# Hybrid encoder block: PSUM banks divided four and four, merge products in both sets by turns, early feature blocks two by two

## The chip, the cores and the metric

The kernel runs on one core of a Trainium2 chip. The metric is the device time of one execution in microseconds (us). Five engines work side by side: TensorE (PE, matrix products and transpositions), VectorE (DVE), ScalarE (ACT), GpSimd (POOL) and SyncE (SP), which here issues the DMAs. Each takes its instructions in the order of its own queue and waits on semaphores for the others. PE accumulates into banks of PSUM; this kernel uses eight tiles of 128 x 512 float32 there.

## The reference

The reference is an encoder block of 1024 tokens and model width 1024: a projection, two attention branches, a gated merge, an output projection, and a SwiGLU feed-forward of width D_FF = 2816. The part that the change touches begins behind the attention branches:

```python
    merged = jax.nn.sigmoid(ga) * (y_a @ w_ba) + jax.nn.sigmoid(gb) * (y_b @ w_bb)
    return merged @ w_o

def swiglu(h, w_gate, w_up, w_down):
    return (jax.nn.silu(h @ w_gate) * (h @ w_up)) @ w_down
```

Around the feed-forward stand a residual sum, an RMS norm ahead of it and one at the end.

## The kernel before

Each float32 operand is split into a high and a low part, and a product of two operand tiles is three matmuls (high by high, high by low, low by high).

**Merge** (`gated`, tile names ppa). There are 32 products: 8 output blocks `o` by 2 token halves, first for branch b (i = 0), then for branch a (i = 1). Each loads its gate from memory into one of four gate tiles (gt), ACT applies the sigmoid, PE makes 12 matmuls into a bank, DVE multiplies gate and bank (L896), and for branch a POOL adds that to the sum (L897), which also frees the gate tile. Branch a runs half 0 mostly first: the last six of its sixteen products are blocks 2 to 7 of half 1. Sums and differences of merged blocks (L905, L912, L913, L1159) and of weights (L1107, L1161, L1163) for the next stage stand on DVE between these.

**Output projection** (po) is done by a Strassen-Winograd scheme of seven block products. Products 1 and 2 accumulate into four banks each (set1, set2), later ones follow in the same sets; products 5 and 3 take a third set of four. `out_add` (L934) adds a finished bank to the residual h. When a row block of h is complete, `norm_f` makes its norm xn_f (L1062, L1064) and stores h.

**Turns** (`turn_f`, tile names ptn_f) transpose xn_f on PE: eight transpositions of a row block into two banks, from which ACT and DVE make the operands b11, b21, b22 and, for row blocks 4 to 7, the sums t (L1082 to L1097). Turns 5, 6 and 7 stand between the first feed-forward products: ahead of products number 0, 2 and 4.

**Feed-forward gate and up** (`product_f`, tile names pg) goes over 11 blocks of 256 features (fp), again with seven block products p in the order 1, 2, 6, 5, 7, 3, 4, each for gate (i = 0) and up (i = 1). One product is 12 matmuls. The result of p = 1 is needed twice: as the first part of p = 2's bank and of p = 6's bank. ACT therefore copies it (L1239) into a second bank. The first four blocks do their p = 1 and p = 2 ahead of the rest, since the operands of the other products are not ready. Of these four, the first N_KEPT keep the p = 1 bank until p = 6; the others ("late") copy p = 1 to a tile in SBUF, let p = 2 accumulate on the same bank, and copy the tile back to a new bank when p = 6 comes. A finished gate block goes through Silu on ACT (L1227); the up block is multiplied in by DVE (L1232). Weights come through raw tiles (five, shared with xn_f), are split by ACT and by DVE or POOL (L112, L113), and wait in eight operand tiles (wop).

**Down projection** (pd, `product_d`) is one more Winograd scheme with sets of four banks.

PSUM for all of this is one pool with two tags: `ps_bank`, six tiles, and `ps_bank_t`, two tiles. The transpositions use ps_bank_t, the feed-forward's products ps_bank except p = 5. A tile is given to a new user when its last user is done.

PE's order is the order in which the program is written. The order on the other engines from the merge to the end of the feed-forward's gate and up part is set by the framework's scheduler, from its own model; from the down projection on it is the written order again.

Of the kernel before, what the change touches and what calls it, by code (L numbers as in the profile page):

```python
# [70 lines left out]
def encoder_block(ctx: ExitStack, tc: tile.TileContext, x, meta, norm_mix, w_in, lq1, lk1, lq2, lk2,  # L71
# [10 lines left out]
    def pool(name, side="left", space=None, bufs=1):  # L82
        kw = {} if space is None else {"space": space}
        if space is not DRAM:
            kw["reuse_waits"] = "tile"
        cm = tc.tile_pool(name=name, bufs=bufs, side=side, **kw)
        p = cm.__enter__()
        return p, lambda: cm.__exit__(None, None, None)
# [5 lines left out]
    def bank(p, tag, name, bufs):  # L94
        return p.tile([P, 512], F32, tag=tag, name=name, bufs=bufs)
# [452 lines left out]
    def branch_mm(ps, w, src, tk):  # L548
        for j in range(4):
            for n, (a, b) in enumerate(((0, 0), (0, 1), (1, 0))):  # L550
                nc.tensor.matmul(ps, w[:, a, j, :], src(j, b, tk),
                                 start=(j == 0 and n == 0), stop=(j == 3 and n == 2))
# [208 lines left out]
    psum3, close_psum3 = pool("psum3", space=PSUM)  # L761
# [1 line left out]


    def ps_bank(name):
        return bank(psum3, "bank", name, 6)

    def ps_bank_t(name):
        return bank(psum3, "bank_t", name, 2)

    pad, close_pad = pool("pad", "right")
    pad.tile([P, PAD // 4], F32, name="pad")
# [83 lines left out]
    def gated(i, o, half, w, src):  # L856
        tk = slice(half * 512, half * 512 + 512)
        gt = ypool.tile([P, 512], F32, tag="gt", name=f"gt_{i}_{o}_{half}", bufs=GT_BUFS)
        nc.sync.dma_start(gt, g_d[8 * i + o][:, tk])
        nc.scalar.activation(gt, gt, AF.Sigmoid)  # L860
        ps = (ps_bank_t if half else ps_bank)(f"ppa_{o}_{half}_{i}")
        branch_mm(ps, w, src, tk)
        return gt, ps, tk

# [2 lines left out]
    for o in range(DC):  # L867
        w = first_w[o] if o < 2 else branch_w(ypool, o, w_bb, "b")
        for half in range(2):
            gt, ps, tk = gated(0, o, half, w, yb)  # L870
            nc.vector.tensor_tensor(merged(o, half), gt, ps, ALU.mult)
        if o in (1, 5):
            load_ya(o // 4)
        if 3 <= o < 6:
            load_wo(*((w11, 0, 0), (w12, 0, 1), (w21, 1, 0))[o - 3])
        if o >= 4:
            right_o(1, o - 4)
            tt_v(w11[:, o - 4], w12[:, o - 4], w11[:, o - 4], ALU.subtract)
        if o == 6:
            ws_a = {0: branch_w(ypool, 0, w_ba, "a", None, nc.vector)}  # L880
        if 2 <= o < 6:
            split_ya(0, o - 2)
# [9 lines left out]
    for n, (o, half) in enumerate(order_a):  # L892
        if o not in ws_a:
            ws_a[o] = branch_w(ypool, o, w_ba, "a", None, nc.vector)
        gt, ps, tk = gated(1, o, half, ws_a[o], ya)
        nc.vector.tensor_tensor(gt, gt, ps, ALU.mult)  # L896
        nc.gpsimd.tensor_tensor(merged(o, half), gt, merged(o, half), ALU.add)  # L897
        if 4 <= n < 8:
            right_o(2, n - 4)
            left_o(1, n - 4)  # L900
        elif 10 <= n < 14:
            left_o(2, n - 10)
        if n in (6, 8, 10, 11):

            tt_v(a21[:, o], a11[:, o], a21[:, o], ALU.subtract)  # L905
        if n == 10:
            w22 = obpools["w22"] = block_pair(2, "m2", F32)[:, 0]
            load_wo(w22, 1, 1)
        if n >= 12:

            j = n - 12
            tt_v(asum[:, j], a22[:, j], a21[:, j], ALU.subtract)  # L912
            tt_v(a11[:, j], asum[:, j], a11[:, j], ALU.add)  # L913
# [18 lines left out]
    def out_add(t, q, ps):  # L932
        cols = slice(q * 512, q * 512 + 512)
        nc.vector.tensor_tensor(h2[t][:, cols], h2[t][:, cols], ps, ALU.add)  # L934

    first, rest, order_pm = (1, 2), (6, 5, 7, 3, 4), (1, 2, 6, 5, 7, 3, 4)
    N_EARLY, N_KEPT = 4, 2
    order_f = [(0, p, i) for p in first for i in range(2)]
    order_f += [(fp, p, i) for fp in range(1, N_EARLY) for i in range(2) for p in first]
    order_f += [(fp, p, i) for fp in range(N_EARLY) for p in rest for i in range(2)]  # L940
    order_f += [(fp, p, i) for fp in range(N_EARLY, NJ) for p in first + rest for i in range(2)]
    nf = len(order_f)
# [116 lines left out]
    def norm_f(t):  # L1059
        xn = raw_tile(f"xn_f{t}")  # L1060
        ss = small.tile([P, 1], F32, tag="ss", name=f"ss_f{t}")
        nc.scalar.activation(xn, h2[t], AF.Square, accum_out=ss)  # L1062
        r = rstd_of(ss, D, P, f"rstd_f{t}")
        nc.vector.scalar_tensor_tensor(xn, h2[t], r, gffn, ALU.mult, ALU.mult)  # L1064
        nc.sync.dma_start(h2_d[t], h2[t])
        xns[t] = xn

    def turn_f(t):
# [5 lines left out]
        for b in range(2):  # L1074
            pt = four(ps_bank_t(f"ptn_f{t}_{b}"))
            for c in range(4):
                k = 4 * b + c
                nc.tensor.transpose(pt[:, c, :], xn[:, k * P:(k + 1) * P], ident)
            pts.append(pt)
            if b or not half:  # L1080
                op = b22 if half else (b11, b21)[b]
                nc.scalar.activation(op[:, 0, :, cols], pt, AF.Copy)  # L1082
                nc.vector.tensor_tensor(op[:, 1, :, cols], pt, f32(op[:, 0, :, cols]), ALU.subtract)
            if not half:
                nc.scalar.copy(four(kept[:, b * 512:b * 512 + 512]), pt)
# [23 lines left out]
    order_t = ((7, 0), (7, 1), (7, 2), (4, 0), (7, 3), (4, 1), (4, 2), (4, 3))  # L1109
    steps_o = [(p, j) for p in (1, 2, 6, 5, 3) for j in range(4)]  # L1110
    set1 = [ps_bank(f"po_1_{u}") for u in range(4)]
    set2 = [(ps_bank, ps_bank_t)[u // 2](f"po_2_{u}") for u in range(4)]
    sets_o = {1: set1, 2: set2, 6: set1}

    def product_o(p, j, u):
        oa, ob = lefts[p, j], rights[p, j]
        for k, (a, b) in enumerate(((0, 0), (0, 1), (1, 0))):
            nc.tensor.matmul(sets_o[p][u], oa[:, a, u * P:(u + 1) * P], ob[:, b, :],  # L1118
                             start=(p in (1, 5) and j == 0 and k == 0),
                             stop=(p in (2, 3) and j == 3 and k == 2), skip_group_check=True)  # L1120
# [8 lines left out]
    def ahead(n):  # L1129

        if n + 8 < 20:
            p, j = steps_o[n + 8]
            right_o(p, j)
            left_o(p, j)
        else:
            right_o((7, 4)[n // 4 - 3], n % 4)
            left_t(*order_t[n - 12])

    for n, (p, j) in enumerate(steps_o):
        if (p, j) == (5, 0):  # L1140
            sets_o[5] = sets_o[3] = [(ps_bank, ps_bank_t)[u // 2](f"po_5_{u}") for u in range(4)]
        last = p in (5, 3) and j == 3
        if p in (5, 3) and j == 2:
            continue
        for u in range(4):
            for k in (2, 3) if last else (j,):
                product_o(p, k, u)
            if (p, j) == (1, 3):

                nc.scalar.copy(set2[u], set1[u])  # L1150
            elif j == 3:

                out_add(u + 4 * (p == 5), int(p > 2), sets_o[p][u])
                if p == 3:
                    norm_f(u)
        for k in (n - 1, n) if last else (n,):
            ahead(k)
            if 4 <= k < 8:
                tt_v(a12[:, k - 4], a12[:, k - 4], asum[:, k - 4], ALU.subtract)  # L1159
            elif 8 <= k < 12:  # L1160
                tt_v(w12[:, k - 8], w22[:, k - 8], w12[:, k - 8], ALU.subtract)  # L1161
            elif 12 <= k < 16:
                tt_v(w21[:, k - 12], w21[:, k - 12], t2[(k - 12) // 2][:, k % 2 * 512:k % 2 * 512 + 512], ALU.subtract)  # L1163
# [134 lines left out]
    sums, sets = {}, {}  # L1298
    BANKS = {1: 1, 6: 1, 7: 1, 4: 1, 2: 2, 5: 5, 3: 5}
# [4 lines left out]
    def product_d(p, j, us_):  # L1304
        oa, ob = ops["d", (p, j)]
        if BANKS[p] not in sets:
            sets[BANKS[p]] = [(ps_bank_t if BANKS[p] > 1 and u > 1 else ps_bank)(f"pd_{p}_{u}") for u in range(4)]
        ps = sets[BANKS[p]]
        for u in us_:
            for k, (a, b) in enumerate(((0, 0), (0, 1), (1, 0))):  # L1310
                nc.tensor.matmul(ps[u], oa[:, a, u * P:(u + 1) * P], ob[:, b, :],  # L1311
                                 start=(p in (1, 2, 5) and j == 0 and k == 0),
                                 stop=(p in (2, 3, 4) and j == NJ - 1 and k == 2), skip_group_check=True)
# [53 lines left out]
    for n in range(nf, len(steps)):  # L1367
        p, j = steps[n][1]
# [3 lines left out]
        if p in LOADS:  # L1372
            at, half, col = LOADS[p]
# [62 lines left out]
```

## Time and profile before

| What | Value |
|---|---|
| Three timed runs | 1477.86, 1481.01, 1481.19 us (median 1481.01) |
| Profiled execution | 1472.57 us, span 1470.8 us |
| Granted TensorE clock, mean of the span | 0.991 |
| Busy: PE, DVE, ACT, POOL | 1439.6, 895.4, 676.0, 474.1 us |
| The output projection begins | 730.36 us |
| The feed-forward's first product begins | 814.46 us |
| Its block products from p = 6 on begin | 876.98 us |
| The down projection begins | 1252.34 us |

The span runs from the first to the last instruction of the profiled execution. A row of a timeline gives start, length, engine, line, operation, output and inputs, form and count, and in brackets the time that the engine stood idle before it and what ended the idling. A row of the waits names engine, tile and line, what it waited for, then the sum, the number and the longest. Tile names in the profile leave the numbers out: pg is any product bank of the feed-forward, wop any weight operand, p the SBUF tile of p = 1.

### The profile page before, as it was taken

What the parts mean: (1) busy time and instruction counts of PE and PEld (TensorE: products, weight loads), DVE (VectorE), ACT (ScalarE), POOL (GpSimd) and SP (SyncE); (2) the same over time, 40 slices, a digit from 0 to 9 for tenths busy, and PEclk for the clock granted to TensorE, in tenths of its full rate; (3) what the DMA queues carried; (4) which work ended last, traced back from release to release, by engine and by line L of the source; (5) the groups of instructions that cost most, each with busy time, mean ns of one, the idle gap of its engine ahead of it and who ended that gap; (6) DMA issues with size and microseconds to landing.
All of it is one profiled execution on the core that took longest, in us unless ns stands there. A gap on an engine that the chain in (4) does not pass through costs nothing.

```text
span 1470.8 us, 20980 instructions
## 1 busy us (share of the span) xinstructions
PE 1439.6 (98%) x7327; PEld 1232.8 (84%) x7327; DVE 895.4 (61%) x1750; ACT 676.0 (46%) x1273; POOL 474.1 (32%) x460
## 2 busy tenths in 40 slices
PE   8999999999999999999899799999999999999997
PEld 7999989988898989888688578888888888888886
DVE  6456326628686878346777835564444443787667
ACT  6356336526455545356246634333333333444454
POOL 4143223313322322222403024555455442000444
PEclk9999999999999999999999899999999999999999
DMA  7333452372524151195232524333333323954343
GB/s 234 90 98 113 118 130 85 77 228 77 145 73 152 66 152 66 43 343 172 95 143 86 165 79 129 123 123 107 108 101 100 102 94 106 347 197 141 125 128 137
DMA packets 158617, 191.01 MB, mean 130 GB/s; under 512 B 16096, under 2 KB 103584, under 8 KB 158512
## 3 DMA queue, kind: packets, MB, share of 16 engines
q1 hardware_dynamic: 158512, 189.68, 40.8%
q8 instruction: 58, 0.95, 0.3%
q14 instruction: 47, 0.39, 0.1%
HBM read 129.14 MB, written 53.94 MB: 124 GB/s over the span
## 4 chain that ended last, share of the span: by engine, by line
PE 82%; DMA 4%; issue 4%; POOL 3%; DVE 3%; ACT 2%; SPq 0%; POOLq 0%; ACTq 0%; DVEq 0%
PE pg L1215 28%; PE pp_g L200 11%; PE pd L1311 8%; PE aps L607 4%; PE po L1118 3%; PE apy L649 3%; PE pp_qb L200 3%; PE pp_va L200 3%; PE pp_ka L200 3%; PE pp_qa L200 3%; POOL oa L113 3%; PE apt L636 2%; PE bpt L338 2%; PE bpy L344 2%; PE bps L313 1%
## 5 line engine op out<-in xcount | busy, mean ns | idle before, releaser
L1215 PE MATMUL pg<-t,wop 128*128 128x512 f32 x1056 | 242.4, 389 | 0.0
L1215 PEld LDWEIGHTS pg<-t,wop 128*128 128x128 f32 x1056 | 198.2, 188 | 41.2
L1311 PE MATMUL pd<-ob,oa 128*128 128x512 f32 x924 | 210.2, 389 | 0.9 <-DVE ob L113 0.5
L113 POOL TENSOR_TENSOR wop<-wf,wop 128x512 fp32r<-128x512 f32 x114 | 153.3, 1345 | 165.5 <-ACT wop L112 153.7
L1311 PEld LDWEIGHTS pd<-ob,oa 128*128 128x128 f32 x924 | 173.3, 188 | 37.6 <-DVE ob L113 0.9
L1215 PE MATMUL pg<-b,wop 128*128 128x512 f32 x792 | 187.9, 395 | 4.0 <-ACT p L1239 2.7
L1215 PEld LDWEIGHTS pg<-b,wop 128*128 128x128 f32 x792 | 150.2, 191 | 37.8 <-ACT p L1239 4.4
L113 POOL TENSOR_TENSOR wl_c<-w_c,wh_c 128x1024 fp32r<-128x1024 f32 x32 | 77.7, 2428 | 162.0 <-ACT wh_c L112 151.8
L112 ACT ACTIVATE wop<-wf 128x512 fp32r<-128x512 f32 x128 | 80.6, 632 | 79.5 <-PE pg L1215 46.8
L618 ACT ACTIVATE as<-as,amn 128x1040 f32<-128x1040 f32 x64 | 74.6, 1165 | 72.6 <-DVE amn L613 72.4
L200 PE MATMUL pp_g<-hT_hi,wh_c 128*128 128x512 f32 x256 | 101.3, 396 | 0.0
L200 PE MATMUL pp_g<-hT_lo,wh_c 128*128 128x512 f32 x256 | 100.9, 394 | 0.0
L200 PE MATMUL pp_g<-hT_hi,wl_c 128*128 128x512 f32 x256 | 100.9, 394 | 0.0
L113 POOL TENSOR_TENSOR oa<-ra,oa 128x512 fp32r<-128x512 f32 x33 | 44.1, 1337 | 170.8 <-ACT oa L112 169.3
L112 ACT ACTIVATE oa<-ra 128x512 fp32r<-128x512 f32 x77 | 48.7, 632 | 106.7 <-PE pd L1311 51.4
L607 PE MATMUL aps<-ak,aq 128*128 128x352 f32 (+1 forms) x384 | 92.6, 326 | 0.0
L987 DVE TENSOR_TENSOR s<-wf,wf 128x512 f32<-128x512 f32 x22 | 17.1, 779 | 123.0 <-DMA wf<-in_w_ff_up_dram 73.6
L607 PEld LDWEIGHTS aps<-ak,aq 128*128 128x128 f32 x384 | 69.6, 188 | 14.0
L613 DVE CUSTOM_DVE_ANT_0 as<-aps,dist,amn 128x352 f32<-128x352 f32 (+1 forms) x128 | 71.3, 563 | 10.2 <-PE aps L607 8.1
L325 POOL TENSOR_SCALAR bs<-bs,bdn 128x432 f32<-128x432 f32 (+1 forms) x64 | 37.2, 600 | 88.1 <-DVE bdn L323 65.3
L315 DVE CUSTOM_DVE_ANT_0 bs<-bps,tbx,nsink 128x432 f32<-128x432 f32 (+1 forms) x64 | 38.4, 624 | 41.4 <-PE bps L313 38.3
L621 POOL TENSOR_SCALAR as<-as,adn,neglam 128x1040 f32<-128x1040 f32 x32 | 39.0, 1220 | 75.2 <-DVE adn L619 75.2
(270 smaller groups left out, 3047.2 us busy)
## 6 DMA issues: line engine op xcount, KB each, us to landing
ra<-aop SPq DMA_DIRECT2D x77, 256.0 KB, 2.7
w_c<-in_w_in_dram SPq DMA_DIRECT2D x33, 512.0 KB, 4.2
wf<-in_w_ff_gate_dram SPq DMA_DIRECT2D x25, 512.0 KB, 3.8
wf<-in_w_ff_up_dram SPq DMA_DIRECT2D x25, 512.0 KB, 3.8
aop<-as SPq DMA_DIRECT2D x44, 256.0 KB, 2.1
aop<-c SPq DMA_DIRECT2D x33, 256.0 KB, 2.0
g_d<-gate_stage SPq DMA_DIRECT2D x32, 256.0 KB, 2.0
gt<-g_d SPq DMA_DIRECT2D x32, 256.0 KB, 4.2
```

The lines of the kernel that those rows point to most:

```text
L112: nc.scalar.activation(hi, src, AF.Copy)
L113: lo_eng.tensor_tensor(lo, src, f32(hi), ALU.subtract)
L200: nc.tensor.matmul(ps[:, :n], a[:, c, :], b[:, c, at:at + n], start=(c == 0 and i == 0), stop=(c == DC - 1 and i == 2))
L315: nc.vector.tensor_tensor_reduce(st[:, r, :W], ps[:, :W], tb, 2.0 ** -(4 * g + r + 1), nsink[:, 4 * g + r:4 * g + r + 1], ALU.add, ALU.min ...
L607: nc.tensor.matmul(ps[:, :n], qs[m][:, t * P:(t + 1) * P], ks[m][:, vv, k0:k0 + n], start=(vv == 0), stop=(vv == 1))
L613: nc.vector.tensor_tensor_reduce(s[m][:, a:b], ps[:, a - k0:b - k0], far_by, slope, low, ALU.add, ALU.min, mn[:, m, i + j:i + j + 1])
L618: nc.scalar.activation(s[m][:, 0:L], s[m][:, 0:L], AF.Exp, bias=low, scale=-1.0, accum_out=dn[:, m:m + 1])
L621: (nc.gpsimd if t % 4 in COMBINE_POOL else nc.vector).tensor_scalar(s[1][:, 0:L], s[1][:, 0:L], dn[:, 1:2], neglam, ALU.mult, ALU.mult)
L649: nc.tensor.matmul(py[:, cols], v[:kp, a, k, :], at_[:kp, k, b, :], start=(k == 0 and j == 0), stop=(k == 8))
L1118: nc.tensor.matmul(sets_o[p][u], oa[:, a, u * P:(u + 1) * P], ob[:, b, :], start=(p in (1, 5) and j == 0 and k == 0), stop=(p in (2, 3) an ...
L1215: nc.tensor.matmul(ps, op[:, x, c, :], b[:, y, c, :], start=(p in (1, 5) and c == 0 and n == 0), stop=(p in (4, 2, 3) and c == 3 and n == ...
L1311: nc.tensor.matmul(ps[u], oa[:, a, u * P:(u + 1) * P], ob[:, b, :], start=(p in (1, 2, 5) and j == 0 and k == 0), stop=(p in (2, 3, 4) and ...
```

## The change

- The eight banks are divided four and four: ps_bank has four tiles, ps_bank_t four.
- Products of the merge take a tile of either set by turns, by a count over all 32, instead of by token half.
- The second and third set of the output projection and the sets 2 and 5 of the down projection lie wholly in ps_bank_t.
- In the feature blocks 1 to 3 the order is p = 1 gate, p = 1 up, p = 2 gate, p = 2 up, instead of p = 1, p = 2 of gate and then of up.
- N_KEPT goes from 2 to 1, so that block 1 is "late" too: its p = 1 goes through an SBUF tile. That adds two ACT copies of 128 x 512 (from SBUF to a bank, ahead of its p = 6).

```diff
@@ -763,10 +763,12 @@
 
 
     def ps_bank(name):
-        return bank(psum3, "bank", name, 6)
+        return bank(psum3, "bank", name, 4)
+
+    n_gated = [0]
 
     def ps_bank_t(name):
-        return bank(psum3, "bank_t", name, 2)
+        return bank(psum3, "bank_t", name, 4)
 
     pad, close_pad = pool("pad", "right")
     pad.tile([P, PAD // 4], F32, name="pad")
@@ -858,7 +860,8 @@
         gt = ypool.tile([P, 512], F32, tag="gt", name=f"gt_{i}_{o}_{half}", bufs=GT_BUFS)
         nc.sync.dma_start(gt, g_d[8 * i + o][:, tk])
         nc.scalar.activation(gt, gt, AF.Sigmoid)
-        ps = (ps_bank_t if half else ps_bank)(f"ppa_{o}_{half}_{i}")
+        n_gated[0] += 1
+        ps = (ps_bank_t if n_gated[0] % 2 else ps_bank)(f"ppa_{o}_{half}_{i}")
         branch_mm(ps, w, src, tk)
         return gt, ps, tk
 
@@ -934,9 +937,9 @@
         nc.vector.tensor_tensor(h2[t][:, cols], h2[t][:, cols], ps, ALU.add)
 
     first, rest, order_pm = (1, 2), (6, 5, 7, 3, 4), (1, 2, 6, 5, 7, 3, 4)
-    N_EARLY, N_KEPT = 4, 2
+    N_EARLY, N_KEPT = 4, 1
     order_f = [(0, p, i) for p in first for i in range(2)]
-    order_f += [(fp, p, i) for fp in range(1, N_EARLY) for i in range(2) for p in first]
+    order_f += [(fp, p, i) for fp in range(1, N_EARLY) for p in first for i in range(2)]
     order_f += [(fp, p, i) for fp in range(N_EARLY) for p in rest for i in range(2)]
     order_f += [(fp, p, i) for fp in range(N_EARLY, NJ) for p in first + rest for i in range(2)]
     nf = len(order_f)
@@ -1109,7 +1112,7 @@
     order_t = ((7, 0), (7, 1), (7, 2), (4, 0), (7, 3), (4, 1), (4, 2), (4, 3))
     steps_o = [(p, j) for p in (1, 2, 6, 5, 3) for j in range(4)]
     set1 = [ps_bank(f"po_1_{u}") for u in range(4)]
-    set2 = [(ps_bank, ps_bank_t)[u // 2](f"po_2_{u}") for u in range(4)]
+    set2 = [ps_bank_t(f"po_2_{u}") for u in range(4)]
     sets_o = {1: set1, 2: set2, 6: set1}
 
     def product_o(p, j, u):
@@ -1138,7 +1141,7 @@
 
     for n, (p, j) in enumerate(steps_o):
         if (p, j) == (5, 0):
-            sets_o[5] = sets_o[3] = [(ps_bank, ps_bank_t)[u // 2](f"po_5_{u}") for u in range(4)]
+            sets_o[5] = sets_o[3] = [ps_bank_t(f"po_5_{u}") for u in range(4)]
         last = p in (5, 3) and j == 3
         if p in (5, 3) and j == 2:
             continue
@@ -1304,7 +1307,7 @@
     def product_d(p, j, us_):
         oa, ob = ops["d", (p, j)]
         if BANKS[p] not in sets:
-            sets[BANKS[p]] = [(ps_bank_t if BANKS[p] > 1 and u > 1 else ps_bank)(f"pd_{p}_{u}") for u in range(4)]
+            sets[BANKS[p]] = [(ps_bank_t if BANKS[p] > 1 else ps_bank)(f"pd_{p}_{u}") for u in range(4)]
         ps = sets[BANKS[p]]
         for u in us_:
             for k, (a, b) in enumerate(((0, 0), (0, 1), (1, 0))):
```

Line numbers grow by two behind the first hunk and by three behind the second: L896 is L899 in the changed kernel, L934 is L937, L1082 to L1097 are L1085 to L1100, L1118 is L1121, L1215 is L1218, L1227 is L1230, L1232 is L1235 and L1239 is L1242.

**DVE at the end of the merge.** gt_1_4_1 is the gate of branch a (1), block 4, half 1; m_21, m_22, m0 and m1 are merged blocks and their sums. Before:

```order
L896 TENSOR_TENSOR gt_1_4_1_7543<-gt_1_4_1_7543,ppa_4_1_1_7546 128x512
L905 TENSOR_TENSOR m_21_6840<-m0_6842,m_21_6840 128x512
L912 TENSOR_TENSOR m0_6842<-m_22_6841,m_21_6840 128x512
L913 TENSOR_TENSOR m0_6842<-m0_6842 128x512
L1159 TENSOR_TENSOR m1_6843<-m1_6843,m0_6842 128x512
L896 TENSOR_TENSOR gt_1_5_1_7566<-gt_1_5_1_7566,ppa_5_1_1_7569 128x512
L912 TENSOR_TENSOR m0_6842<-m_22_6841,m_21_6840 128x512
L913 TENSOR_TENSOR m0_6842<-m0_6842 128x512
L1159 TENSOR_TENSOR m1_6843<-m1_6843,m0_6842 128x512
L896 TENSOR_TENSOR gt_1_6_1_7589<-gt_1_6_1_7589,ppa_6_1_1_7592 128x512
L896 TENSOR_TENSOR gt_1_7_1_7609<-gt_1_7_1_7609,ppa_7_1_1_7612 128x512
```

Changed:

```order
L899 TENSOR_TENSOR gt_1_4_1_7543<-gt_1_4_1_7543,ppa_4_1_1_7546 128x512
L899 TENSOR_TENSOR gt_1_5_1_7566<-gt_1_5_1_7566,ppa_5_1_1_7569 128x512
L908 TENSOR_TENSOR m_21_6840<-m0_6842,m_21_6840 128x512
L899 TENSOR_TENSOR gt_1_6_1_7589<-gt_1_6_1_7589,ppa_6_1_1_7592 128x512
L915 TENSOR_TENSOR m0_6842<-m_22_6841,m_21_6840 128x512
L899 TENSOR_TENSOR gt_1_7_1_7609<-gt_1_7_1_7609,ppa_7_1_1_7612 128x512
L916 TENSOR_TENSOR m0_6842<-m0_6842 128x512
L1162 TENSOR_TENSOR m1_6843<-m1_6843,m0_6842 128x512
L915 TENSOR_TENSOR m0_6842<-m_22_6841,m_21_6840 128x512 x2
```

The multiplications of blocks 5, 6 and 7, which release their banks, stand four, six and five rows further ahead, between the sums for the output projection.

**PE at the start of the feed-forward.** ptn_f7 is turn 7; pg_0_1_1 is the bank of gate (0), block 1, p = 1, and wop_0_1_2 the weight of gate, block 1, p = 2; b11 and b21 are the operands of p = 1 and p = 2. Before:

```order
L1078 MATMUL ptn_f7_1_8578<-ident_99,xn_f7_8403 128x128 x4
L1215 MATMUL pg_0_1_1_8591<-b11_8186,wop_0_1_1_8442 128x512 x12
L1215 MATMUL pg_0_1_2_8604<-b21_8187,wop_0_1_2_8445 128x512 x12
L1215 MATMUL pg_1_1_1_8632<-b11_8186,wop_1_1_1_8450 128x512 x12
L1215 MATMUL pg_1_1_2_8645<-b21_8187,wop_1_1_2_8453 128x512 x12
L1215 MATMUL pg_0_2_1_8676<-b11_8186,wop_0_2_1_8491 128x512 x12
L1215 MATMUL pg_0_2_1_8676<-b21_8187,wop_0_2_2_8509 128x512 x12
```

Changed:

```order
L1081 MATMUL ptn_f7_1_8578<-ident_99,xn_f7_8403 128x128 x4
L1218 MATMUL pg_0_1_1_8591<-b11_8186,wop_0_1_1_8442 128x512 x12
L1218 MATMUL pg_1_1_1_8615<-b11_8186,wop_1_1_1_8447 128x512 x12
L1218 MATMUL pg_0_1_1_8591<-b21_8187,wop_0_1_2_8450 128x512 x12
L1218 MATMUL pg_1_1_1_8615<-b21_8187,wop_1_1_2_8453 128x512 x12
L1218 MATMUL pg_0_2_1_8676<-b11_8186,wop_0_2_1_8491 128x512 x12
L1218 MATMUL pg_1_2_1_8706<-b11_8186,wop_1_2_1_8511 128x512 x12
```

The products of gate and up alternate, and both p = 2 products of block 1 accumulate on the bank of p = 1. The count of matmuls is the same.

**ACT at the same place.** wf0_1 and wf1_1 are the raw weights of block 1, gate and up; pg_1_0_2 is the second bank of block 0, up. Before (the table load and the Silu of block 0 come three rows after the last one here):

```order
L1239 COPY pg_0_0_2_8487<-pg_0_0_1_8474 128x512
L112 ACTIVATE wop_0_1_1_8442<-wf0_1_8440 128x512
L112 ACTIVATE wop_0_1_2_8445<-wf0_1_8440 128x512
L1239 COPY pg_1_0_2_8507<-pg_1_0_1_8494 128x512
L112 ACTIVATE wop_1_1_1_8450<-wf1_1_8448 128x512
L112 ACTIVATE wop_1_1_2_8453<-wf1_1_8448 128x512
L112 ACTIVATE t_7_8432<-kept_1_8266 128x4x128
L112 ACTIVATE wop_0_2_1_8491<-wf0_2_8489 128x512
L112 ACTIVATE wop_0_2_2_8509<-wf0_2_8489 128x512
L1097 COPY ts_1_8468<-ptn_f5_1_8461 128x512
L112 ACTIVATE t_4_8433<-kept_1_8266 128x4x128
L112 ACTIVATE t_6_8431<-ts_1_8468 128x4x128
```

Changed:

```order
L1242 COPY pg_0_0_2_8487<-pg_0_0_1_8474 128x512
L112 ACTIVATE t_5_8430<-ts_1_8468 128x4x128
L112 ACTIVATE wop_0_1_1_8442<-wf0_1_8440 128x512
L112 ACTIVATE wop_1_1_1_8447<-wf1_1_8445 128x512
L112 ACTIVATE wop_0_1_2_8450<-wf0_1_8440 128x512
L112 ACTIVATE wop_1_1_2_8453<-wf1_1_8445 128x512
L1242 COPY pg_1_0_2_8507<-pg_1_0_1_8494 128x512
L1085 ACTIVATE b22_8188<-ptn_f6_1_8519 128x4x128
L112 ACTIVATE wop_0_2_1_8491<-wf0_2_8489 128x512
L112 ACTIVATE wop_1_2_1_8511<-wf1_2_8509 128x512
L1230 ACT_TABLE_LOAD
L1230 ACTIVATE c_0_0_11_8548<-pg_0_0_2_8487 128x512
```

The copy to pg_1_0_2 now stands behind all four weight copies of block 1. The Silu of block 0 stands behind the first weight copies of block 2, gate and up, and ahead of the other copies for turns 5 and 6 except the first ones.

## The prediction

> **What bounds the kernel now.** I read first the busy totals, then the table of waits of TensorE (PE), then stretches of the span, then the timelines around the waits.
>
> ```profile
> span 1470.8 us, 20980 instructions
> PE 1439.6 (98%) x7327; PEld 1232.8 (84%) x7327; DVE 895.4 (61%) x1750; ACT 676.0 (46%) x1273; POOL 474.1 (32%) x460
> ```
> ```profile
> PE ptn_f L1078 <- ACT ts L1097: 8.4, 3, 4.9
> PE ppa L551 <- DVE gt L896: 5.3, 1, 5.3
> PE pg L1215 <- ACT p L1239: 2.7, 4, 0.7
> PE pg L1215 <- ACT pg L1239: 1.3, 2, 0.7
> PE ptn_f L1078 <- ACT kept L1085: 0.5, 1, 0.5
> ```
> ```profile
> 720.00:740.00 20.00, 19.76 (x79) 16.01 (x80) 17.10 (x25) 4.22 (x8) 7.95 (x5) 0.90 0.35 125
> 820.00:830.00 10.00, 5.08 (x18) 4.06 (x17) 10.00 (x16) 6.98 (x13) 0.00 (x0) 0.66 0.74 196
> 900.00:950.00 50.00, 50.00 (x223) 41.39 (x222) 31.34 (x36) 19.02 (x33) 25.43 (x19) 1.00 0.44 141
> 1250.00:1300.00 50.00, 49.54 (x219) 40.70 (x218) 37.25 (x59) 21.30 (x36) 0.00 (x0) 1.00 0.98 354
> ```
>
> In a stretch the columns are length, busy us (and count) of PE, weight loads, DVE, ACT and POOL, then the granted clock, DMA share and GB/s. PE is the bound: 50.00 of 50 us from 900 to 950, at clock 1.00. The change issues the same matmuls, so it can win only PE's idle time and the clock lost behind it. All five waits listed (18.2 us) lie at two places, around 715 and 797 to 877. At both the clock falls too (0.90 and 0.66).
>
> ```profile
> 720.24 10.28 PE L551 MATMUL ppa<-ya,wbha 128*128 128x512 f32 x36 [5.25 <-DVE gt L896]
> 730.36 4.92 PE L1118 MATMUL po<-ob_o,oa_o 128*128 128x512 f32 x21
> 814.05 0.66 PE L1078 MATMUL ptn_f<-ident,xn_f 128*128 128x128 f32 x4 [1.09 <-ACT ts L1097]
> 814.46 5.73 PE L1215 MATMUL pg<-b,wop 128*128 128x512 f32 x24
> 825.55 1.11 PE L1078 MATMUL ptn_f<-ident,xn_f 128*128 128x128 f32 x4 [4.92 <-ACT ts L1097]
> 826.32 7.29 PE L1215 MATMUL pg<-b,wop 128*128 128x512 f32 x24
> 836.40 1.07 PE L1078 MATMUL ptn_f<-ident,xn_f 128*128 128x128 f32 x4 [2.35 <-ACT ts L1097]
> 837.12 4.29 PE L1215 MATMUL pg<-b,wop 128*128 128x512 f32 x12
> 842.08 5.74 PE L1215 MATMUL pg<-b,wop 128*128 128x512 f32 x24 [0.66 <-ACT pg L1239]
> 874.13 3.02 PE L1215 MATMUL pg<-b,wop 128*128 128x512 f32 x12 [0.68 <-ACT p L1239]
> 876.98 5.38 PE L1215 MATMUL pg<-t,wop 128*128 128x512 f32 x23
> ```
>
> A product is 12 matmuls: 50 us / 222 x 12 = 2.70 us in an unbroken stream. Three products at 720.24 take 10.12 us to the next row instead of 8.1, so 2.0 us are lost to the clock. Likewise 24 matmuls take 5.73 us after a gap of 1.09, but 7.29 after 4.92 (1.6 lost), and 12 take 4.29 instead of 3.02 after 2.35 (1.3 lost).
>
> **Merge and start of the output projection.** The products of half 1 share two banks, and the bank's release waits in DVE's queue:
>
> ```profile
> 713.48 2.50 DVE L1107 TENSOR_TENSOR t<-m,m 128x512 f32<-128x512 f32 x4 [1.29 <-DMA m<-in_w_out_dram]
> 719.51 0.68 DVE L896 TENSOR_TENSOR gt<-gt,ppa 128x512 f32<-128x512 f32 x1
> 721.91 0.68 DVE L896 TENSOR_TENSOR gt<-gt,ppa 128x512 f32<-128x512 f32 x1
> 730.80 1.27 DVE L896 TENSOR_TENSOR gt<-gt,ppa 128x512 f32<-128x512 f32 x2
> ```
> ```profile
> 725.92 0.63 ACT L860 ACTIVATE gt<-gt 128x512 f32<-128x512 f32 x1 [10.48 <-DMA gt<-g_d]
> ```
>
> By turns, the last products find free banks among eight. PE stops at 720.24 - 5.25 = 714.99; three products follow at once and end at 723.1. The projection then wants four banks of the set of four. Three come from products evacuated by about 723.2 (the 719.51 row, and gt_5_1, now directly behind the 721.91 row, at about 722.5). The fourth needs gt_7_1. Its gate is ready at 726.55 (row 725.92; its load waits for a gate buffer, which this change leaves alone), and DVE's multiplication ends at 727.2. The projection's first three accumulations (3 x 3 matmuls, 2.0 us) fill 723.1 to 725.1, and PE stands 2.1 us. So that a part of the stall moves from L551 to L1118. Before, the fourth accumulation began at 730.36 + 2.0 = 732.4; now at 727.3. **Gain 5.1 us, less up to 1.3 of clock** (the row after 2.35 us idle): I take 4.5.
>
> **Turns and early feature blocks.** From the end of the 814.05 row's predecessor (814.05 - 1.09 = 812.96) to 876.98 there are 64.0 us, with 20 transposes (about 0.1 us each: 814.05 to 814.46 for four) and 16 products: 2.0 + 16 x 2.70 = 45.2 us of work, **18.8 us of excess**. What remains of it depends on ACT and DVE:
>
> ```profile
> 820.32 1.15 ACT L112 ACTIVATE wop<-wf 128x512 fp32r<-128x512 f32 x2 [2.24 <-DMA wf<-in_w_ff_gate_dram]
> 822.12 1.15 ACT L112 ACTIVATE wop<-wf 128x512 fp32r<-128x512 f32 x2 [0.17 <-DMA wf<-in_w_ff_up_dram]
> 830.95 1.28 ACT L1227 ACT_TABLE_LOAD   x1 [3.39 <-PE pg L1215]
> 832.24 0.60 ACT L1227 ACTIVATE c<-pg 128x512 f32<-128x512 f32 x1
> 841.45 0.57 ACT L1239 COPY pg<-pg 128x512 f32<-128x512 f32 x1 [3.05 <-PE pg L1215]
> 854.25 0.59 ACT L1239 COPY p<-pg 128x512 f32<-128x512 f32 x1 [2.08 <-PE pg L1215]
> ```
> ```profile
> 809.51 3.01 PE L1126 MATMUL po<-ob_o,oa_o 128*128 128x512 f32 x12
> ```
> ```profile
> 814.45 0.68 DVE L934 TENSOR_TENSOR h<-h,po 128x512 f32<-128x512 f32 x1
> ```
> ```profile
> DMA to landing us min/median/max: 4.1/6.0/6.7
> ```
>
> The last row is the weight loads wf between 812 and 835. In the clock of before:
> - Four transposition banks let a turn start while the last but one is still being evacuated: the 8.4 us behind L1097 go. Turn 5 ends at 813.4; block 0's first products run to 818.8, turn 6 to 819.6, the second products to 825.0, turn 7 to 825.8.
> - The last of block 0's products needs an ACT copy that now stands behind all four weight copies of block 1. Their loads go out behind the store of h, whose sum (row 814.45) is three DVE operations (2.4 us) earlier in the order, and 1.8 in time, since its matmuls end only at 809.51 + 3.01. The up load then lands at 820.3 instead of 822.1 (row 822.12); three copies at 0.55 and the copy of 0.57 end at 822.6, wanted at 822.3: **stall 0.3 us** (0 to 1).
> - Block 1's first product needs the bank that block 0's Silu frees. On ACT that Silu now stands behind a weight copy whose load is issued when turn 6 ends (its raw buffer): 819.7 + 5.4 (middle of 4.1 and 6.7) = 825.1, copy 0.6, table load 1.28, Silu 0.60: 827.6. **Stall 1.8 us** (0.5 to 3.1). Before, ACT's own queue put it at 832.8.
> - Block 1's second product needs block 0's multiplication on DVE, three operations behind that Silu: about 830.1, and PE wants it at 830.3. No stall.
> - From there two by two: the copy of 0.57 to 0.59 us (rows 841.45, 854.25) lies under another product of 2.70, so the six gaps of 0.66 to 0.68 go. Block 2's second product waits for block 1's multiplication, 21 operations later in DVE's queue: 21 x 0.60 (their spacing: 820 to 830 is 10.00 busy with 16) = 12.6, so 842.7, against 841.2 wanted: **stall 1.5 us** (0 to 5, if a weight load that lands late stands in that queue). Block 3: 0.3 (0 to 1.8).
> - The two added ACT copies (0.6 us each, for block 1 now moved through SBUF) lie in ACT's free time (2 us idle ahead of each copy row above).
>
> Stalls 0.3 + 1.8 + 1.5 + 0.3 = 3.9 us, clock behind them about 1 (0 to 3: the gap of 1.09 cost nothing, that of 2.35 cost 1.3). Gain 18.8 - 4.9 = 13.9. The 0.5 us behind L1085 go with the third and fourth bank. I take 13.5 for both, since 55 DVE operations without a gap have no reserve.
>
> [...]
>
> **The steady part.** With four product banks instead of six, a block's second first-product waits for the Silu of the block before:
>
> ```profile
> 983.26 0.60 ACT L1227 ACTIVATE c<-pg 128x512 f32<-128x512 f32 x1 [2.03 <-PE pg L1215]
> 988.70 0.57 ACT L1239 COPY pg<-pg 128x512 f32<-128x512 f32 x1 [2.03 <-PE pg L1215]
> ```
> ```profile
> 1252.34 4.01 PE L1311 MATMUL pd<-ob,oa 128*128 128x512 f32 x17
> 1252.61 0.69 DVE L1232 TENSOR_TENSOR c<-c,pg 128x512 f32<-128x512 f32 x1 [1.58 <-PE pg L1215]
> ```
>
> That Silu ends at 983.86; the product whose copy starts at 988.70 began its successor at about 988.3: 4.4 us of reserve. The down projection's fourth bank is free at 1253.3 and wanted at 1252.34 + 2.0 = 1254.4: 1.1 us. I cost both at nothing (bounds 0 to 2 us). All later transfers are released by PE's progress and move along.
>
> **Sum.** 4.5 + 13.5 = 18 us; the profiled execution, 1472.57 us (span 1470.8), would become 1454.6. The three timed runs lie at 1477.86 to 1481.19, median 1481.01; against that median 1463.0.
>
> **Rivals.**
> - DVE and the weight loads bind between 811 and 845. For: 10.00 of 10 us busy, loads of up to 6.7 us. Against: only weight operands and a few sums stand there, and none of the four stalls above exceeds 2. Stalls of 11 to 12 instead of 3.9 leave a total gain of about 10: 1471. Chance 0.2.
> - The banks don't do what they should: merge only hands its stall to L1118, and the turns wait for xn_f or ACT instead. Only the six gaps (4.0) and a little clock go: gain 4 or less, 1477 to 1481, within measurement. Chance 0.06.
> - Slower: four banks bind in every later block. It decides once Silu or multiplication come more than 4.4 us late, as they would where DVE stands behind a weight load. Seven blocks at 2.35 + 1.3 us (row 836.40) are 25.6, less 18: 1489. Against: 50.00 of 50 busy leaves ACT 31 us and DVE 19 of 50 free. Chance 0.04.
> - The gain is given back where DMA is full (0.98, 354 GB/s at 1250): if these loads set the end, up to all 18 us, 1481. Against: PE 49.54 of 50 busy there. Chance 0.02.
>
> **How the numbers follow.** Forecast 0.68. The range 1455 to 1474 takes in 26 us (all excess of both places, 18.8 + 7.3) and the first rival down to a gain of 7. Below 0.3% (4.4 us) a measurement of this kernel cannot tell a change from none. Faster 0.88 (forecast and first rival), same 0.08, slower 0.04.
>
> **What would show it.** In the waits of PE the rows L1078 behind L1097 and L551 behind L896 must be gone; the rows of L1218 behind the copies too. New and short: L1121 behind DVE L899 (about 2 us), L1218 behind ACT L1230 and DVE L1235 (1 to 2 each). From 812 on the early blocks' last product should end some 14 us sooner relative to the projection. I am wrong if L1218 shows a wait in block after block beyond 880, or if a wait of more than 4 us stands at 825 to 845.

## The result

The changed kernel takes 1455.26 us (median of 6 runs, 1451.94 to 1459.43) against 1477.18 us before (median of 6, 1472.15 to 1481.19). The ratio is 0.9853, with a 95% interval of 0.9827 to 0.9879: faster by 1.5%. The profiled execution took 1455.01 us with a span of 1453.2, so 17.6 us less than the span of before. Measured again later, the changed kernel stood at 0.9865 (0.9848 to 0.9883), 1454.2 against 1473.4.

The profile after, with the busy totals first, then PE's waits, and then stretches of the span (length, busy us of PE, weight loads, DVE, ACT and POOL with counts, clock, DMA share, GB/s):

```profile
span 1453.2 us, 20988 instructions
PE 1432.0 (99%) x7327; PEld 1227.8 (84%) x7327; DVE 893.5 (61%) x1750; ACT 675.6 (46%) x1275; POOL 471.6 (32%) x460
```
```profile
PE po L1121 <- DVE gt L899: 3.4, 1, 3.4
PE apt L636 <- DVE as L624: 2.1, 1, 2.1
PE pg L1218 <- DVE c L1235: 1.8, 2, 1.4
```
```profile
820.00:830.00 10.00, 9.27 (x43) 7.23 (x43) 10.00 (x18) 9.53 (x17) 0.00 (x0) 1.00 0.63 182
900.00:950.00 50.00, 50.00 (x222) 41.40 (x222) 29.86 (x33) 19.89 (x35) 26.06 (x19) 1.00 0.41 137
1250.00:1300.00 50.00, 50.00 (x222) 41.40 (x221) 39.39 (x64) 23.18 (x40) 0.00 (x0) 1.00 0.80 286
```

The 8.4 us of L1078 behind L1097 and the 5.3 of L551 are gone, and the clock from 820 to 830 is 1.00 instead of 0.66. New is a wait of 3.4 us at the first set of the output projection. The feature blocks from 900 on show no wait with four product banks, nor does the stretch from 1250. PE's timeline shows where time was won:

```profile
723.90 2.20 PE L1121 MATMUL po<-ob_o,oa_o 128*128 128x512 f32 x9
729.48 5.77 PE L1121 MATMUL po<-ob_o,oa_o 128*128 128x512 f32 x17 [3.38 <-DVE gt L899]
```
```profile
810.73 5.71 PE L1218 MATMUL pg<-b,wop 128*128 128x512 f32 x24
816.27 1.04 PE L1081 MATMUL ptn_f<-ident,xn_f 128*128 128x128 f32 x8
817.07 3.01 PE L1218 MATMUL pg<-b,wop 128*128 128x512 f32 x12
820.41 3.02 PE L1218 MATMUL pg<-b,wop 128*128 128x512 f32 x12 [0.34 <-ACT pg L1242]
823.27 1.03 PE L1081 MATMUL ptn_f<-ident,xn_f 128*128 128x128 f32 x8
824.24 3.04 PE L1218 MATMUL pg<-b,wop 128*128 128x512 f32 x12
827.67 11.17 PE L1218 MATMUL pg<-b,wop 128*128 128x512 f32 x48 [0.39 <-DVE c L1235]
840.28 19.36 PE L1218 MATMUL pg<-b,wop 128*128 128x512 f32 x84 [1.44 <-DVE c L1235]
859.47 10.81 PE L1218 MATMUL pg<-t,wop 128*128 128x512 f32 x47
```

The feed-forward begins 3.7 us sooner than before (814.46, now 810.73), and the products from p = 6 on 17.5 us sooner (876.98, now 859.47). From there on nothing more is won or lost. Of the 3.7 us, 2.6 are won at the turns ahead of the feed-forward, which begin with these rows, before and after:

```profile
792.92 1.04 PE L1078 MATMUL ptn_f<-ident,xn_f 128*128 128x128 f32 x8
```
```profile
791.77 1.04 PE L1081 MATMUL ptn_f<-ident,xn_f 128*128 128x128 f32 x8
```

From there to 814.46 and 810.73 it is 21.5 us before and 19.0 now: the waits of 0.5 and 1.1 are gone, and 1.0 more because the other transpositions follow one another without delay. So the turns and early blocks gave 13.8 + 2.6 = 16.4 us, of which 1.0 lies in places that the prediction did not count. The other 1.1 us of the 3.7 are the merge's. Its branch a began 0.9 us later on PE than before (680.33 against 679.47), most of it at the merge's start, behind the wait of 2.1 us for L636, which is no part of the change (below); counted from there, the merge gave 2.0.

### The profile page after: what moved, and what is told of

It reads as the page before. It is cut to its first block, busy times and chain, and to the rows that moved or that the text cites. A ratio compares the mean times of both kernels' runs of the same rounds, so it can differ in the third digit from the quotient of the medians.

```text
span 1453.2 us, 20988 instructions
## 1 busy us (share of the span) xinstructions
PE 1432.0 (99%) x7327; PEld 1227.8 (84%) x7327; DVE 893.5 (61%) x1750; ACT 675.6 (46%) x1275; POOL 471.6 (32%) x460
## 4 chain that ended last, share of the span: by engine, by line
PE 81%; DMA 6%; issue 4%; POOL 4%; DVE 3%; ACT 2%; SPq 1%; POOLq 0%; ACTq 0%; DVEq 0%
PE pg L1218 28%; PE pp_g L200 10%; PE pd L1314 8%; PE aps L607 4%; PE po L1121 4%; PE apy L649 3%; PE pp_va L200 3%; PE pp_ka L200 3%; PE pp_qa L200 3%; PE pp_qb L200 3%; POOL oa L113 3%; PE apt L636 2%; PE bpt L338 2%; PE bpy L344 2%; PE po L1129 2%
## 5 line engine op out<-in xcount | busy, mean ns | idle before, releaser
L1218 PE MATMUL pg<-t,wop 128*128 128x512 f32 x1056 | 242.4, 389 | 0.0
L1218 PEld LDWEIGHTS pg<-t,wop 128*128 128x128 f32 x1056 | 198.3, 188 | 41.1
L1218 PE MATMUL pg<-b,wop 128*128 128x512 f32 x792 | 184.2, 390 | 2.2 <-DVE c L1235 1.8
L1218 PEld LDWEIGHTS pg<-b,wop 128*128 128x128 f32 x792 | 148.2, 188 | 34.2 <-DVE c L1235 2.7
L112 ACT ACTIVATE oa<-ra 128x512 fp32r<-128x512 f32 x77 | 48.7, 632 | 108.1 <-PE pd L1314 51.3
L613 DVE CUSTOM_DVE_ANT_0 as<-aps,dist,far_a 128x352 f32<-128x352 f32 x64 | 37.1, 579 | 42.8 <-PE aps L607 42.7
```

The source lines that it names most:

```text
L112: nc.scalar.activation(hi, src, AF.Copy)
L613: nc.vector.tensor_tensor_reduce(s[m][:, a:b], ps[:, a - k0:b - k0], far_by, slope, low, ALU.add, ALU.min, mn[:, m, i + j:i + j + 1])
L1218: nc.tensor.matmul(ps, op[:, x, c, :], b[:, y, c, :], start=(p in (1, 5) and c == 0 and n == 0), stop=(p in (4, 2, 3) and c == 3 and n == ...
```

## The experiments

All are built from the changed kernel; "span" is that of the profiled execution. Two profiled executions of the changed kernel itself differ by 2.6 us (1453.2 and 1450.6), so a difference of a few us is read from the waits and from the interval of the ratio rather than from the span.

**Merge by halves on four and four banks.**

```diff
-        ps = (ps_bank_t if n_gated[0] % 2 else ps_bank)(f"ppa_{o}_{half}_{i}")
+        ps = (ps_bank_t if half else ps_bank)(f"ppa_{o}_{half}_{i}")
```

> The changed kernel, but with the merge's products put by token half again (half 1 in the second set, now of four banks). Theory A, the merge needs four banks for half 1 and not the turns: the last product waits about 0.5 us for block 3's multiplication, and the projection's first set is free, so that the stall of 3.4 us at L1121 and the 1.7 us of clock behind it go: span 1453.2 - 4.6 = 1448.6, ratio to before near 0.982. Theory B, the turns removed the stall of 5.3 us: it comes back with its clock loss, 7.3 us in place of 5.1, span about 1455.5.

Measured: span 1449.2, ratio 0.9836 (0.9823 to 0.9849). PE's timeline there:

```profile
713.77 11.68 PE L551 MATMUL ppa<-ya,wbha 128*128 128x512 f32 x50
725.29 11.04 PE L1121 MATMUL po<-ob_o,oa_o 128*128 128x512 f32 x48
```

The merge runs into the projection without a gap; not even the 0.5 us show. So Theory A holds: it was the number of banks for half 1 that removed the old stall. Taking turns put block 7's product of half 1 into a bank that the projection wants fourth, and costs 4.0 us of span against halves, 0.3% by the ratios (0.9836 against 0.9865, whose intervals just touch); from the merge's first product to the feed-forward's it is 4.5 (169.8 against 174.3 us). One wait is there that the changed kernel does not have, for block 0's Silu:

```profile
PE pg L1218 <- ACT c L1230: 1.1, 1, 1.1
```

**The old order in the blocks 1 to 3.**

```diff
-    order_f += [(fp, p, i) for fp in range(1, N_EARLY) for p in first for i in range(2)]
+    order_f += [(fp, p, i) for fp in range(1, N_EARLY) for i in range(2) for p in first]
```

> The changed kernel, but the feature blocks 1 to 3 in the order of before (p = 1, p = 2 of gate, then of up). Theory A, the two-by-two order hides the copy of p = 1: six waits of 0.66 us behind L1242 come back, 4.0 us, with their drained pipelines about 5.2, while the two waits of L1218 behind L1235 (1.8 us) go: span 1453.2 + 3 = 1456 to 1457. Rival, the waits behind DVE's multiplication were the same time under another name: span within 1 us of 1453.2.

Measured: span 1457.7, ratio 0.9879 (0.9862 to 0.9896). Its waits and one of the six gaps:

```profile
PE pg L1218 <- ACT p L1242: 4.8, 6, 1.4
```
```profile
835.37 5.74 PE L1218 MATMUL pg<-b,wop 128*128 128x512 f32 x24 [0.68 <-ACT p L1242]
```

The copies show again in every pair, and the waits for DVE's multiplication are gone, as Theory A has it. A gap of 0.68 costs more than itself there: the starts of two pairs lie 6.41 us apart (835.37 and 841.78), against 5.44 for 24 matmuls without a gap (1036.25 and 1041.69 in the second of the two clock kernels below), so 0.97. The 4.5 us of span are more than the waits account for (4.8 in place of 2.1 us). From the feed-forward's first product to p = 6 it took 52.1 us (811.80 to 863.87) instead of 48.7, so the order is worth 3.3 there; the rest was lost ahead of it, where the clock behind L1121 was halved for 6.8 us instead of 3.4. The interval of the ratio overlaps with that of the changed kernel: that the order helps is shown by the waits and this stretch, not by the times.

**Six and two banks.** The edit sets the two counts back to 6 and 2 and the merge, output and down projection to their banks of before.

```diff
-        return bank(psum3, "bank", name, 4)
+        return bank(psum3, "bank", name, 6)
...
-        return bank(psum3, "bank_t", name, 4)
+        return bank(psum3, "bank_t", name, 2)
```

> The changed kernel with six and two banks again, and with merge, output and down projection on the banks of before; so only the order of blocks 1 to 3 and N_KEPT = 1 of the change are left. Theory A, the second set of four is what frees the turns: the waits of L1081 behind L1100 come back (8.4 us, some 3 of clock) and so does the merge's (7.3 in place of 5.1): span 1453.2 + 13 = 1466. Rival, the turns' waits came from DVE's and ACT's queues: they stay gone, and the span is about 1456.

Measured: span 1466.6, ratio 0.9964 (0.9952 to 0.9977). Its waits:

```profile
PE ppa L551 <- DVE gt L899: 7.2, 1, 7.2
PE ptn_f L1081 <- DVE ts L1096: 6.3, 2, 3.3
...
PE ptn_f L1081 <- ACT ts L1100: 1.1, 1, 1.1
```

Both stalls are back with the small second set. (That most of the turns' wait now ends with DVE's L1096 and not ACT's copy is the other reader of the same two banks.) What is left of the change there, the order and N_KEPT = 1, is worth 4.2 us; the previous run, which has the banks without the order, 13.1. The sum, 17.3, is close to the whole, 17.6 (by the ratios 0.4 and 1.2% against 1.3 to 1.5), but not because each part is the same everywhere: with six and two banks what is left of the change saves 5.9 us from the feed-forward's first product to p = 6 (56.6 us against 62.5 before), and the merge's stall is 2 us longer than before. The parts add to within a few us, no closer.

**Halves, and block 2's late banks in the second set.**

```diff
-            u[which] = (ps_bank_t if p == 5 else ps_bank)(f"pg_{nm}_{p}")
+            u[which] = (ps_bank_t if p == 5 or (fp == 2 and p == 1) else ps_bank)(f"pg_{nm}_{p}")
```

> As e1_halves, and the two late banks of feature block 2 lie in the second set, which is free there. Theory A: beside the 4.6 us of the merge the wait of block 2's second product for the multiplication (1.44 us) goes: span 1453.2 - 6 = 1447. Rival, DVE's queue of some 55 operations is the limit: the wait moves to block 3 and only the merge's gain is seen, 1448.6.

Measured: median 1446.75 us, span 1445.8, ratio 0.9821 (0.9808 to 0.9835). This beats both kernels: its interval lies below that of the changed kernel's second measurement (0.9848 to 0.9883) and overlaps by a little with that of its first (0.9827 to 0.9879). No row of L1218 behind L1235 is left, and what remains in these blocks is

```profile
PE pg L1218 <- ACT pg L1242: 0.7, 1, 0.7
...
PE pg L1218 <- ACT c L1230: 0.2, 1, 0.2
```

So a bank that is free already removes the wait of 1.44 us though DVE is no faster, and it did not move to block 3. Whether a faster DVE would do the same was not tried.

**The changed kernel again**, beside the next two:

> The changed kernel itself, in the same call as the next three. Theory A: the saving is what its profile shows, 17.5 us: 0.988 of before. Rival: the undisturbed runs gain more than the profiled ones, about 22 us, 0.985.

Measured: 0.9865 (0.9848 to 0.9883), span 1450.6. The interval holds both, 0.988 and 0.985. The second profiled execution is 20.2 us below the one of before, the first 17.6, which is the same spread; the two theories are not told apart. In this second one the wait of L636 ahead of the merge (2.1 us) is absent: it comes and goes between executions of one and the same kernel, and is none of the change.

**Five gate tiles**, with merge by turns, and with halves and block 2's late banks in the second set:

```diff
-GT_BUFS = 4
+GT_BUFS = 5
```

> The changed kernel with five gate tiles instead of four. Theory A: the stall of 3.4 us at L1121 is block 7's multiplication, held by its late gate (728.08) for about 1.2 us, the rest by DVE's queue, so that some 2.2 us of it stay, too short for the clock to fall: gain 1.2 + 1.7, span about 1450.3. Rival, the gate alone holds it: stall below 0.5, span 1448. Rival, DVE's queue alone: stall 3.4, span 1453.

> As e4_best (merge by halves, block 2's banks in the second set), with five gate tiles. Theory A: no merge product waits there for its gate any more, so nothing changes: span 1446 +- 1. Rival: the projection's operands come earlier and PE's small waits go: 1445.

Measured: span 1462.5 and ratio 0.9918 (0.9903 to 0.9933) with turns; 1455.5 and 0.9891 (0.9872 to 0.9911) with halves. Both are slower than the same kernel with four, by 9 to 12 us of span, which no theory had said. The waits of the first:

```profile
PE ppa L551 <- ACT yb L112: 8.1, 1, 8.1
...
PE po L1121 <- DVE gt L899: 2.3, 1, 2.3
```

The stall in question did fall, to 2.3, as Theory A had it, but it was not too short for the clock: behind 2.28 us the clock fell to 0.50, which cost 1.7, where the changed kernel's gap of 2.15 us at L636, ahead of nine transpositions, had cost none (1.00 from 336 to 344). But a stall of 8.1 us appears at the start of the merge. ACT's timeline shows it, first of this kernel, then of the changed one:

```profile
638.80 3.30 ACT L862 ACTIVATE gt<-gt 128x512 f32<-128x512 f32 x5 [0.73 <-DMA gt<-g_d]
...
643.56 4.26 ACT L112 ACTIVATE yb<-m 128x512 fp32r<-128x512 f32 x8
```
```profile
635.12 3.25 ACT L112 ACTIVATE yb<-m 128x512 fp32r<-128x512 f32 x5 [0.24 <-DMA m<-yb_d]
...
640.16 2.19 ACT L862 ACTIVATE gt<-gt 128x512 f32<-128x512 f32 x4
```

With a fifth tile the scheduler put five sigmoids, which wait for their loads, ahead of the splits of yb that PE's first product needs.

**The clock behind a gap.** Each of these two kernels ran once, profiled (spans 1482.7 and 1469.9); only the rows behind the gaps are used. A chain of ACT copies, started by the last product of the block before, ends in the bank that a block's first product uses (or, in the variant with transpositions, in a spare bank that four transpositions write, with four more ahead of the gap). The copies and transpositions compute nothing that is used.

```diff
+        if p == 1 and i == 0 and fp in PROBE:
+            nc.scalar.copy(s[0], prev)
+            for k in range(1, n_c):
+                nc.scalar.copy(s[k % 2], s[(k + 1) % 2])
...
+            nc.scalar.copy(ps, s[(n_c + 1) % 2])
```

> The changed kernel with PE made to wait, by a chain of ACT copies behind the last product of the block before, ahead of the first product of the feature blocks 5 to 10; it adds copies, and transpositions of the identity into spare banks, that nothing uses. Blocks 5 and 7: four copies, a gap of about 2.3 us between matmuls. Blocks 6 and 8: the same gap with four transpositions ahead of it and four behind it, about 3.3 us without a matmul. Block 9: seven copies, a gap of about 3.8 us without transpositions. Block 10: two copies, 1.3 us, with transpositions, 2.3 without a matmul. [...] Theory B (the prediction's charge), an idle gap of 2.3 us is enough: 5, 6, 7, 8 and 9 all lose 1.3 us or more.

> As e7_clock, with shorter gaps and no transpositions: two copies ahead of blocks 5, 7 and 9, three ahead of 6, 8 and 10 (a copy of the chain took 0.65 us there: gaps of about 2.1 and 2.7 us). [...] Theory B, a gap of 2.3 us always costs: the three of 2.7 all lose 1.7.

A copy of the chain took 0.65 us instead of 0.5, so that the gaps came out longer. PE's timeline, first kernel (blocks 5 to 10), then two of the six gaps of the second:

```profile
1006.26 12.63 PE L1237 MATMUL pg<-b,wop 128*128 128x512 f32 x48 [3.39 <-ACT pg L1231]
...
1049.49 0.66 PE L1226 MATMUL probe_u<-ident 128*128 128x128 f32 x4 [2.95 <-ACT probe_u L1224]
1049.90 12.75 PE L1237 MATMUL pg<-b,wop 128*128 128x512 f32 x48
...
1093.23 12.82 PE L1237 MATMUL pg<-b,wop 128*128 128x512 f32 x48 [3.39 <-ACT pg L1231]
...
1137.41 13.57 PE L1237 MATMUL pg<-b,wop 128*128 128x512 f32 x48
...
1183.51 12.72 PE L1237 MATMUL pg<-b,wop 128*128 128x512 f32 x48 [5.33 <-ACT pg L1231]
...
1225.53 0.66 PE L1226 MATMUL probe_u<-ident 128*128 128x128 f32 x4 [1.65 <-ACT probe_u L1224]
1225.94 11.17 PE L1237 MATMUL pg<-b,wop 128*128 128x512 f32 x48
```
```profile
1008.90 11.19 PE L1237 MATMUL pg<-b,wop 128*128 128x512 f32 x48 [2.09 <-ACT pg L1231]
1050.03 11.20 PE L1237 MATMUL pg<-b,wop 128*128 128x512 f32 x48 [2.74 <-ACT pg L1231]
```

48 matmuls at the full clock take 11.2 us. Gaps of 2.09 and 2.74 (three of each) cost nothing; by Theory B the three of 2.74 would have lost 1.7 each. Two gaps of 3.39 cost 1.4 and 1.6, and one of 5.33 cost 1.5, no more than the shorter ones. 2.95 us with four transpositions on either side, so about 4.0 without a matmul, cost 1.6 and 2.4. A gap of 1.65 with the same transpositions, 2.7 without a matmul, cost nothing. So in the blocks of these two kernels up to 2.74 us without a matmul were free, and 3.39 and more cost 1.4 to 2.4. The stall at L1121, in the merge of these and the other runs, doesn't keep to that: 2.28 us (five gate tiles) and 2.90 (the changed kernel again) each lost 1.7 us to a halved clock, 3.33 (the old order) lost 3.1, while 2.99 (the first of these two kernels) lost none. (These losses are sums over windows of half a us: busy time by the missing share of the clock.) The stretch behind the gap of 2.28, in columns of length, PE's busy us, clock, DMA share and GB/s, and the row behind the gap of 2.99, where 99 matmuls take 0.230 us each, no more than 48 at the full clock (0.233):

```profile
738.00:740.00 2.00, 1.10 (x3) 0.74 0.00 0
740.00:742.00 2.00, 2.00 (x6) 0.50 0.74 199
```
```profile
727.49 22.74 PE L1121 MATMUL po<-ob_o,oa_o 128*128 128x512 f32 x99 [2.99 <-DVE gt L899]
```

So between 2.28 and 2.99 us, with no transpositions beside the gap, the price was 0 or 1.7, and the length alone does not say which. What decides it is not shown.

## Why the prediction was right

The forecast was 1463.0 us against a median of 1481.01, and 1454.6 for the profiled execution. The latter was 1455.01. The median was 1455.26, against a median of before that itself came out 3.8 us lower with six runs; it stands at the lower end of the stated range (1455 to 1474). That the sum met the profiled execution within half a us is luck in part: the merge gave 2.5 us less than forecast, the turns and early blocks 2.9 more, and 0.9 was lost ahead of branch a.

- **That the gain lies in two places and nowhere else**: right. The steady part and the down projection cost nothing, as said; the rival with four banks bound in every block and the one with the gain given back at 1250 are out (50.00 of 50 us busy in both stretches).
- **Merge, 4.5 us**: right in its mechanism, the stall handed in part to L1121, too large in size: 2.0. The term that failed is the wait for gt_7_1, 2.1 us, measured 3.38:

```profile
721.02 0.68 DVE L899 TENSOR_TENSOR gt<-gt,ppa 128x512 f32<-128x512 f32 x1
728.08 0.63 ACT L862 ACTIVATE gt<-gt 128x512 f32<-128x512 f32 x1 [11.03 <-DMA gt<-g_d]
728.74 0.69 DVE L899 TENSOR_TENSOR gt<-gt,ppa 128x512 f32<-128x512 f32 x1 [0.61 <-ACT gt L862]
```

The gate was ready at 728.71, 2.2 us later than the prediction took from the profile of before, while branch a began only 0.9 us later on PE. Two things make up the 1.3. The load reuses a gate tile that comes free behind the multiplication of block 3 (row 721.02, before 719.51) and POOL's sum; that multiplication came 0.65 us later behind the start of branch a. And the load itself took 0.6 us longer, before and after:

```profile
DMA to landing us min/median/max: 2.7/2.7/2.7
```
```profile
DMA to landing us min/median/max: 3.3/3.3/3.3
```

Only the second holds in full in the other profiles with turns and four gate tiles: the load takes 3.4 to 3.5 us in them, while the multiplication comes only 0.05 to 0.4 us later, and the stall is 2.90 to 3.33. The likely reason is that the loads of h now stand right behind the gate's (from 725.11 on), where before they were issued only at 730.59, after a wait for the stalled product:

```profile
SPq L927 <- PE ppa L551: 7.1, 1, 7.1
```

So the stall that went had kept other transfers away from this load; that they are what slows it was not tried. The prediction left the load at its old time. The stall 1.3 us longer and the clock behind it at 1.7 us instead of 0.6 are nearly the whole difference.

- **Turns, Silu and multiplication**: forecast 13.5 (13.9 and 0.5 by its sum), measured 15.4 in the same places. The stall behind the weight copies was 0.34 (forecast 0.3), the one of block 2 behind the multiplication 1.44 (forecast 1.5). The Silu stall of 1.8 did not come: ACT's row

```profile
821.64 0.64 ACT L112 ACTIVATE wop<-wf 128x512 fp32r<-128x512 f32 x1 [0.24 <-DMA wf<-in_w_ff_up_dram]
822.29 1.28 ACT L1230 ACT_TABLE_LOAD   x1
823.59 0.60 ACT L1230 ACTIVATE c<-pg 128x512 f32<-128x512 f32 x1
```

shows the load landed at 821.6. It was issued when turn 6 ended, at 817.3,

```profile
817.34 0.37 SPq L971 DMA_DIRECT2D wf<-in_w_ff_up_dram  x1
```

so it took 4.3 us and not 5.4, and the Silu ended at 824.19, just when PE wanted the bank (row 824.24). That is the smaller part: counted from the feed-forward's first product the Silu came 0.7 us sooner than forecast, and PE wanted the bank 1.1 us later (13.5 us behind that product instead of 12.4), because of the 0.3 us behind the copy and because PE's short pieces take longer than 2.70 us for each product (12 matmuls on their own take 3.0, row 817.07). That the wait is close by is shown by the merge by halves, where it is 1.1 us. The multiplication behind the Silu then came 0.4 late instead of in time. Altogether the excess from the feed-forward's first product to p = 6 is 48.7 - (1.6 + 16 x 2.70) = 3.9 us, forecast 4.9: 2.2 in stalls, about 1.7 at such edges of PE's pieces, which the prediction had at nothing, and none of clock.
- **The clock**, 1 us: wrong here, nothing was lost between 820 and 850 (1.00), behind stalls of 0.34, 0.39 and 1.44 us. The charge rested on the gap of 2.35 us before, which cost 1.3 and had transpositions on both sides: from 833.45 to 837.12 no matmul ran, 3.7 us. In the probes, 2.09 and 2.74 us without transpositions cost nothing, and 2.95 with them, about 4.0 without a matmul, cost 1.6 and 2.4. But the merge's stalls of 2.28 and 2.90 us, without transpositions, lost 1.7 each, so what part the transpositions had in the 1.3 us of before is not shown.
- **DVE as the new bound** (rival): not so. DVE is 10.00 of 10 busy from 820 to 830 and from 830 to 840, but its longest hold on PE there was 1.44 us, and a free bank removes that (the run with block 2 in the second set).

## What to carry to other kernels

When PSUM is divided anew, ask for each bank who takes it next: turns over all banks look even, but they gave the late product a bank that the next stage wanted at once, and plain halves were 4 us better. A stall that goes away lets other work start earlier: ask which transfers it had held back, and what stands beside them, before taking a releaser's time from the old trace (here the load of a gate, 3.3 us instead of 2.7). And change a buffer count with the order of every queue beside it: where a scheduler sets the order, one tile more cost 9 to 12 us at a place some 90 us away.

## What was not expected of the hardware

For the gaps without transpositions beside them that were read in windows of half a us, the loss came in steps and not in proportion. It was 1.4 to 1.7 us, with the clock at 0.50 for 3.4 us, for gaps of 2.28 (five gate tiles), 2.90 and 3.38 (the changed kernel, second and first profile), 3.39 twice and 5.33 (first clock kernel). It was about 3, with 0.50 for 6.8 us, for 3.33 (the old order) and 3.29 (second clock kernel). It was nothing for 2.74 three times over (second clock kernel) and for 2.99 (first). Of the shorter gaps, 2.09 three times over (second clock kernel) and 2.15 (L636 in the changed kernel, ahead of transpositions) cost nothing, and in the profiles before and after no shorter one cost any clock behind the first 25 us of the span.
